# Queries, keys and values as Strassen units of a stage of their own, attention between the gates' products, and down sums that start from nothing

## The chip, the cores and the metric

The kernel runs on one core of a Trainium2 chip. The metric is device time in microseconds, lower is better. Before the change the median of three runs is 2300.4 us (2299.05 to 2302.49).

The engines named in the text: PE multiplies matrices (PEld is its loading of weights), DVE and ACT are the two larger elementwise engines, POOL a smaller one, and SP only issues DMA transfers. Each works through its own instructions in order.

## The reference

One decoder block on 1024 tokens of 1024 features, in fp32:

```python
xn = rmsnorm(x, norm1_g)
qa, ka, va, qr, kr, vr, gr, gate_a, gate_b = [xn @ wl[:, lo:hi] for ...]  # 12 heads of 128 in qa, ka, va
qa, ka = rmsnorm(qa, q_norm_g), rmsnorm(ka, k_norm_g)                      # per head
o_a = mix of three dilated window attentions (4 heads each), weighted by their softmax denominators
o_r = head_groupnorm(retention(qr, kr, vr)) * silu(gr)                     # 4 heads, q and k 256 wide, v 512
y = sigmoid(gate_a) * (o_a @ w_proj_a) + sigmoid(gate_b) * (o_r @ w_proj_b)
x = x + y @ w_out
x = x + square(relu(rmsnorm(x, norm2_g) @ w_up)) @ w_down                  # 4096 wide
```

## The kernel before, in words

**Products.** Each fp32 operand is split in two: h, a copy rounded to a short format (ACT, L319), and l, what is left of it (DVE, L320). A product is then three matmuls, h by h, h by l and l by h (`Pipe.group`, L223). Weights come from DRAM in blocks of 128 x 1024 (`raw`), are split by `Weights.pump`, and keep six pairs of buffers (`wh`, `wl`); a pair is free again when its last product is done (`W.free`).

**Slots.** `Pipe.step` is one slot: the matmuls of one result tile. Small matmuls and transposes that belong to other work are registered with `pipe.at(lag, ...)` and are put between the terms of a later slot ("inserts"). PE's order is the order of the program, written out by hand. The order on the other engines is found by a scheduler when the kernel is built.

**Stages.** (1) Attention: for 12 heads, 8 blocks of 128 tokens each; a step makes q, k and v of one head for one block (8 terms, 24 matmuls of 384 columns), tokens on partitions. q and k are normalised (ACT L651, DVE L332, POOL L333, DVE L655), turned over (two transposes in one insert, L661) and kept in SBUF. Inserts of later slots compute the scores (L585; maximum on DVE L588, exponential on ACT L592), turn them (L598) and multiply them by the values (L605; copied out by ACT, L607). These inserts use the three banks of the PSUM pool `ms`. (2) Gates 0 to 2 as plain products (288 matmuls of 512 columns), beside which DVE makes the sums and differences of x that Strassen's method needs (L715, L718). (3) 21 Strassen units: 5 of gates, 8 of retention's queries and keys, 8 of its swish gates. A unit multiplies in seven products, N1 to N7, of 12 matmuls (`product`); ACT and DVE combine them (L388, L393, L396 on ACT, L398, L403 on DVE), the gates' sigmoid is L690 on ACT, and DVE sums the quarters of the weights (L121). (4) Retention, (5) the projections `w_pa`, `w_pb`, (6) `w_out` with the residual, whose rows are stored to `y_d` in DRAM, (7) the up product and (8) the down product, both by Strassen's method.

**Down sums.** The down product adds its partial products on DVE into eight tiles Y (L1177). Y starts as the residual rows: `load_sums` (L1153) reads them from `y_d`, two tiles while the up product runs and six of 512 KB each at the start of the down product. The finished tiles are stored to `out` by SP in 16 transfers.

Of the kernel before, what the change touches and what calls it, by code (L numbers as in the profile page):

```python
# [17 lines left out]
P = 128  # L18
# [7 lines left out]
RH = 4  # L26
# [11 lines left out]
class Weights:  # L38
# [12 lines left out]
    def __init__(self, nc, rawp, wp, split):  # L51
        self.nc, self.rawp, self.wp, self.split = nc, rawp, wp, split
        self.raw, self.used, self.next = [], set(), 0
        self.src, self.steps = [], []
        self.place, self.more = [], None
# [19 lines left out]
    def add(self, src, buf=None):  # L75
# [17 lines left out]
        self.plain += 1  # L93

# [71 lines left out]
    def load(self):  # L166
# [4 lines left out]
        if any(self.place[m] == b and m not in self.used for m in range(max(0, n - 8), n)):  # L171
            return False
        if b == self.RAW and self.more is None:
            return False
        raw = (self.more if b == self.RAW else self.rawp).tile([P, UW], F, name=f"raw{b}", bufs=1)
# [94 lines left out]
def hybrid_block(ctx: ExitStack, tc: tile.TileContext, a: dict, out: bass.AP):  # L270
# [9 lines left out]
    big = pool(ctx, "big", 4)  # L280
# [14 lines left out]
    v_d = dram.tile([HEADS, S, DH], F, name="v_d")  # L295

    h_d = dram.tile([FF // 512, 2, 4, P, 7, 2, P], F, name="h_d")
    y_d = dram.tile([S, D], F, name="y_d")
# [6 lines left out]
    XS = {(j, i): slot_of(big) for i in range(2) for j in range(2)}  # L305
# [22 lines left out]
    const.tile([P, 224], F, name="rest")  # L328

    def rsqrt(dst, src, scale):  # L330
        w = src.shape[1]
        nc.vector.tensor_scalar(dst, src, scale, EPS, op0=OP.mult, op1=OP.add)  # L332
        nc.gpsimd.tensor_tensor(dst, dst, half[:, :w], op=OP.pow)  # L333
# [7 lines left out]
    for slot, g in heads:  # L341
        for u in range(4):
            W.add(a["w_att"][g * SLOTS + slot, u])
    for d, bufs in enumerate([(0, 1), (2, 4), (3, 5)]):
        for u, b in enumerate(bufs):
            W.add(a["w_gate"][d, u], b)
    NG, NQ = KT - 3, 2 * RH
# [64 lines left out]
    def put_transposed(xn, t, q):  # L412
        pt = tr.tile([P, 4, P], F, name="tr")
        for i in range(4):
            k = 4 * q + i
            nc.tensor.transpose(pt[:, i, :], xn[:, k * P:(k + 1) * P], ident)
        split(*X(slice(4 * q, 4 * q + 4), slice(t * P, (t + 1) * P)), pt)

    def dilated(g, b, src, dst):

        if g == 0:
            return src, dst[:, b * P:(b + 1) * P]
        r = 4 if g == 1 else 8
        src = src.rearrange("p (i r) -> p r i", r=r)
        if g == 1:
            nb, j = divmod(b, 4)
            return src, dst.rearrange("p (r i) -> p r i", r=r)[:, :, nb * P + 32 * j:nb * P + 32 * j + 32]
        return src, dst.rearrange("p (r i) -> p r i", r=r)[:, :, 16 * b:16 * b + 16]

# [61 lines left out]
    attn = ExitStack()  # L491
    p3 = pool(attn, "p3", 2, "right")
    p2 = pool(attn, "p2", 2, "right")
    cpa = pool(attn, "cpa", 1, "right")
    with ExitStack() as ph:
        cp = pool(ph, "cp", 1)
        first = ExitStack()
        px = pool(first, "px", 2)
        cmb = None

        g1 = cp.tile([P, D], F, name="g1")
        gq = cpa.tile([P, HEADS], F, name="gq")
        gk = cpa.tile([P, HEADS], F, name="gk")
        dist = cp.tile([P, 2, 2 * P], F, name="dist")
        row = px.tile([P, D], F, name="xn", bufs=3)
        ones = cp.tile([1, P], F, name="ones")
        xts = {}

        def load_x(t):
            xts[t] = px.tile([P, D], F, name="xt", bufs=3)  # L510
            nc.sync.dma_start(xts[t], a["x"][t * P:(t + 1) * P, :])

        xts[0] = px.tile([P, D], F, name="xt", bufs=3)
        for cs in halves():
# [8 lines left out]
        xn = px.tile([P, D], F, name="xn", bufs=3)  # L523
# [25 lines left out]
        def norm1(t):  # L549
            if t not in xts:  # L550
                load_x(t)
            ss = px.tile([P, 4], F, name="ss")
            xn = px.tile([P, D], F, name="xn", bufs=3)
            nc.scalar.activation(xn, xts[t], AF.Square, accum_out=ss[:, 0:1])
            rsqrt(ss[:, 1:2], ss[:, 0:1], 1.0 / D)
            nc.vector.scalar_tensor_tensor(xn, xts[t], ss[:, 1:2], g1, op0=OP.mult, op1=OP.mult)
            pipe.at(t - 1 - pipe.slot, *[lambda q=q: put_transposed(xn, t, q) for q in range(2)])
# [3 lines left out]
        nc.sync.dma_start(gq, a["q_norm_g"])  # L561
        nc.sync.dma_start(gk, a["k_norm_g"])
        nc.sync.dma_start(dist, a["c_dist"])

        for head, (slot, g) in enumerate(heads):
            h = g * SLOTS + slot
            slope = 2.0 ** (-8.0 * (h + 1) / HEADS)
            us = W.take(4)
            bias = p2.tile([P, 2 * P], F, name="bias")
            qT = p2.tile([P, S], F, name="qT")  # L570
            kT = p2.tile([P, S], F, name="kT")
            V = p2.tile([P, NT, DH], F, name="V")
            Vd = p2.tile([P, NT, DH], F, name="Vd") if g > 0 else V
            acc = p2.tile([P, NT, DH + 2], F, name="acc")

            def attend(g, h, b, bias, qT, kT, V, acc):

                nk = 2 if has_prev(g, b) else 1
                n = nk * P
                k0 = (b + 1 - nk) * P  # L580
                st = {}

                def scores():
                    sp = ms.tile([P, 512], F, name="ms")
                    nc.tensor.matmul(sp[:, :n], qT[:, b * P:(b + 1) * P], kT[:, k0:k0 + n], start=True, stop=True)  # L585
                    s = p3.tile([P, 2 * P], F, name="s")
                    mx = p3.tile([P, 1], F, name="mx")
                    nc.vector.tensor_tensor_reduce(s[:, :n], sp[:, :n], bias[:, 2 * P - n:], op0=OP.add, op1=OP.max,  # L588
                                                   scale=1.0, scalar=-3.0e38, accum_out=mx)
                    nc.vector.tensor_scalar(acc[:, b, DH:DH + 1], mx, -1.0, None, op0=OP.mult)  # L590
                    st["p"] = p3.tile([P, 2 * P], F, name="pr")
                    nc.scalar.activation(st["p"][:, :n], s[:, :n], AF.Exp, bias=acc[:, b, DH:DH + 1],  # L592
                                         accum_out=acc[:, b, DH + 1:DH + 2])

                def turn():
                    tp = ms.tile([P, 512], F, name="ms")
                    for j in range(nk):
                        nc.tensor.transpose(tp[:, j * P:(j + 1) * P], st["p"][:, j * P:(j + 1) * P], ident)  # L598
                    st["t"] = p3.tile([P, 2 * P], F, name="pT")
                    nc.vector.tensor_copy(st["t"][:, :n], tp[:, :n])  # L600

                def values():
# [719 lines left out]
```

## Time and profile before

| | us |
|---|---|
| median of three runs | 2300.4 |
| the profiled execution | 2299.8 |
| its span in the profile | 2297.7 |
| PE busy | 2236.2 |
| DVE busy | 1341.9 |
| ACT busy | 988.0 |
| POOL busy | 103.0 |
| mean granted clock of PE | 0.993 |

In the profile a group of instructions is a line, an engine, an operation and the tiles "out<-in". A wait is written "who <- whom". The attention stage ends near 551 us, the plain gates near 596, the Strassen units near 1000, retention near 1365, the projections near 1596, `w_out` near 1635, the up product near 1985.

### The profile page before, as it was taken

Reading aid. Unit: us, or ns where it says so; the run is one execution under the profiler, and the core shown is the slowest. Engines: PE = TensorE matmul, PEld = TensorE weight load, DVE = VectorE, ACT = ScalarE, POOL = GpSimd, SP = SyncE. Lnnn points to the kernel's source line nnn. Section 1 sums busy time; section 2 is a strip of 40 time slices with the busy share of each in tenths; the row PEclk is TensorE's granted clock in tenths of the full one; section 3 lists DMA queues with packets and bytes.
Section 4 is the critical chain, followed back from the end, with each engine's and each line's share of the span. In section 5 each row is a group of like instructions: output and inputs, shape, how many; then the busy total and the mean of one; then the engine's idle time right before and its main releaser. Section 6 shows DMA issues by size and latency. Waiting matters only on the chain.

```text
span 2297.7 us, 29975 instructions
## 1 busy us (share of the span) xinstructions
PE 2236.2 (97%) x10868; PEld 1915.5 (83%) x10868; DVE 1341.9 (58%) x2588; ACT 988.0 (43%) x2166; POOL 103.0 (4%) x148
## 2 busy tenths in 40 slices
PE   8999999999999999989999999999999999699999
PEld 7999999998888888878888778888787777588887
DVE  6444545455544445548777842453877778777774
ACT  5444435345443333435555533122666667422220
POOL 1111111110000000000000000000000000000000
PEclk9999999999999999999999999999999999899999
DMA  4313132223233333363433484554377789966655
GB/s 146 97 52 114 53 93 93 81 84 101 88 110 110 110 110 110 106 174 111 120 119 101 140 289 152 170 179 142 115 219 230 229 238 277 329 241 261 234 223 201
DMA packets 288805, 353.53 MB, mean 154 GB/s; under 512 B 14609, under 2 KB 215441, under 8 KB 288658
## 3 DMA queue, kind: packets, MB, share of 16 engines
q1 hardware_dynamic: 288658, 351.63, 48.3%
q8 instruction: 85, 1.39, 0.3%
q14 instruction: 62, 0.51, 0.1%
HBM read 229.84 MB, written 121.73 MB: 153 GB/s over the span
## 4 chain that ended last, share of the span: by engine, by line
PE 77%; DVE 8%; DMA 7%; ACT 4%; issue 3%; POOL 0%; SPq 0%; POOLq 0%; ACTq 0%; DVEq 0%
PE mm L223 51%; PE ms L223 20%; DMA raw<-in_w_up 3%; ACT wh L319 2%; DVE wl L320 2%; DMA h_d<-hs 1%; PE ms L605 1%; DVE hs L320 1%; PE ms L585 1%; DVE raw L121 1%; PE tr L661 1%; DVE xl L320 1%; PE ms L598 1%; PE ms L821 1%; DVE u L1120 1%
## 5 line engine op out<-in xcount | busy, mean ns | idle before, releaser
L223 PE MATMUL mm<-wh,xh 128*128 128x384 f32 (+1 forms) x1280 | 503.8, 394 | 0.0
L320 DVE TENSOR_TENSOR wl<-raw,wh 128x1024 fp32r<-128x1024 f32 (+2 forms) x274 | 297.4, 1088 | 298.6 <-ACT wh L319 295.5
L223 PE MATMUL mm<-wh,xl 128*128 128x384 f32 (+1 forms) x1280 | 460.4, 360 | 4.3 <-DVE xl L320 3.2
L223 PE MATMUL mm<-wl,xh 128*128 128x384 f32 (+1 forms) x1280 | 459.2, 359 | 0.0
L319 ACT ACTIVATE wh<-raw 128x1024 fp32r<-128x1024 f32 (+2 forms) x274 | 257.6, 949 | 301.0 <-PE mm L223 77.9
L223 PE MATMUL mm<-xl,wh 128*128 128x512 f32 x848 | 310.0, 390 | 1.7 <-DVE xl L320 1.7
L223 PE MATMUL mm<-xh,wh 128*128 128x512 f32 x848 | 310.5, 391 | 0.0
L223 PE MATMUL mm<-xh,wl 128*128 128x512 f32 x720 | 280.7, 390 | 0.0
L223 PEld LDWEIGHTS mm<-wh,xl 128*128 128x128 f32 x1280 | 241.4, 189 | 27.2 <-DVE xl L320 4.3
L223 PEld LDWEIGHTS mm<-wh,xh 128*128 128x128 f32 x1280 | 242.6, 190 | 21.0 <-ACT ms L1172 0.5
L223 PEld LDWEIGHTS mm<-wl,xh 128*128 128x128 f32 x1280 | 243.4, 190 | 19.1
L223 PE MATMUL ms<-xh,wh 128*128 128x512 f32 x604 | 239.8, 397 | 16.8 <-ACT u L393 13.8
L223 PE MATMUL ms<-xh,wl 128*128 128x512 f32 x604 | 236.0, 391 | 0.0
L223 PE MATMUL ms<-xl,wh 128*128 128x512 f32 x604 | 235.9, 391 | 0.0
L223 PEld LDWEIGHTS mm<-xl,wh 128*128 128x128 f32 x848 | 159.7, 188 | 35.1 <-DVE xl L320 2.1
L223 PEld LDWEIGHTS mm<-xh,wh 128*128 128x128 f32 x848 | 159.7, 188 | 34.0 <-ACT u L396 0.7
L223 PEld LDWEIGHTS mm<-xh,wl 128*128 128x128 f32 x720 | 135.6, 188 | 28.2
L223 PEld LDWEIGHTS ms<-xh,wh 128*128 128x128 f32 x604 | 113.8, 188 | 45.1 <-ACT u L393 18.8
L223 PEld LDWEIGHTS ms<-xh,wl 128*128 128x128 f32 x604 | 113.7, 188 | 24.0
L223 PEld LDWEIGHTS ms<-xl,wh 128*128 128x128 f32 x604 | 113.8, 188 | 22.3
L592 ACT ACTIVATE pr<-s,acc 128x128 f32<-128x128 f32 (+1 forms) x96 | 43.1, 449 | 148.4 <-DVE acc L590 125.5
L1177 DVE TENSOR_TENSOR Y<-Y,ms 128x512 f32<-128x512 f32 x96 | 65.8, 685 | 62.2 <-PE ms L223 62.1
(254 smaller groups left out, 3284.2 us busy)
## 6 DMA issues: line engine op xcount, KB each, us to landing
h_d<-hs SPq DMA_DIRECT2D x112, 512.0 KB, 5.7
xh<-h_d SPq DMA_DIRECT2D x32, 896.0 KB, 5.9
xl<-h_d SPq DMA_DIRECT2D x32, 896.0 KB, 7.2
raw<-in_w_att SPq DMA_DIRECT2D x48, 384.0 KB, 4.0
raw<-in_w_up SPq DMA_DIRECT2D x32, 512.0 KB, 5.1
raw<-in_w_down SPq DMA_DIRECT2D x32, 512.0 KB, 6.0
sg_d<-sg SPq DMA_DIRECT2D x32, 256.0 KB, 2.1
raw<-in_w_rqk_q SPq DMA_DIRECT2D x16, 512.0 KB, 3.7
```

The source lines that it names most:

```text
L121: self.nc.vector.tensor_tensor(x, x, y, op=OP.add)
L223: self.nc.tensor.matmul(ps, x, y, start=start, stop=stop, skip_group_check=not first)
L319: nc.scalar.activation(dst_h, src, AF.Copy)
L320: nc.vector.tensor_tensor(dst_l, src, dst_h.bitcast(F), op=OP.subtract)
L585: nc.tensor.matmul(sp[:, :n], qT[:, b * P:(b + 1) * P], kT[:, k0:k0 + n], start=True, stop=True)
L592: nc.scalar.activation(st["p"][:, :n], s[:, :n], AF.Exp, bias=acc[:, b, DH:DH + 1], accum_out=acc[:, b, DH + 1:DH + 2])
L598: nc.tensor.transpose(tp[:, j * P:(j + 1) * P], st["p"][:, j * P:(j + 1) * P], ident)
L605: nc.tensor.matmul(po[:, :DH], st["t"][:, j * P:(j + 1) * P], V[:, k0 // P + j, :], start=(j == 0), stop=(j == nk - 1))
L661: nc.tensor.transpose(pt[:, j, :], qk[:, j, :], ident)
L821: nc.tensor.matmul(sp[:, :P], kT[:, f], qT[:, f], start=(f == 0), stop=(f == 1))
L1120: nc.vector.tensor_tensor(held[j, x], held[j, x], held[j, y], op=OP.add)
L1177: nc.vector.tensor_tensor(Y[r][:, ns], Y[r][:, ns], ps, op=op)
```

## The change

**A value stage.** The order of the eight token tiles becomes 0, 4, 1, 5, 2, 6, 3, 7. First comes one plain product: the values of the first four heads (8 steps of 24 matmuls of 512 columns). Beside it POOL makes the sums and differences of x, tile by tile (`differences`, 32 operations of 128 x 512), which DVE made in the plain gates. The quarter of x that Strassen's method does not need as an operand (`x01`, 2 MB in its two parts) goes to DRAM and is read back when retention starts.

**A token stage.** The other values and all queries and keys become four Strassen units with tokens on partitions (`add_tokens`, `TOKEN`): 7 products x 4 token tiles x 12 matmuls of 512 columns each. The sums of their weights are made by POOL (32 operations of 128 x 1024), the partial products are combined by ACT and DVE in SBUF, q and k of two heads at a time are normalised (`heads_out`: squares on ACT into PSUM, a reduction on DVE, a power of 128 x 4 and a product of 128 x 512 on POOL), turned over two slots later (`turn_heads`, four transposes in an insert) and written to DRAM (`qk_d`, `v_d`).

**Gates, queries and keys of retention, swish gates** are now all Strassen units, 24 in place of 21. **Attention** runs between their products: block n is begun at slot 4 + 19n/12, with scores, turn and values as inserts at lags 0, 2 and 4. All inserts use the two banks of the pool `tr`. Per pair of blocks SP loads q, k and v and stores the result.

**Down sums.** `y_d` and `load_sums` are gone. `w_out` stores its rows to `out`; of the first chunk, N2, N6, N5 and N4 are copied into Y by ACT; and the finished tiles are added to `out` by 16 DMA transfers that accumulate, issued by POOL.

The core of the diff:

```diff
+    def add_tokens(self, tag, srcs):
...
+            for name, x, need, ends, sums in (
+                    ("N1", "x11", "x11", (), ()), ("N2", "x12", "x12", ("x12",), ()),
+                    ("N6", "x11", "x22", (), (("x22", "x21"), ("x21", "x11"), ("x11", "x22"))),
...
+                            self.nc.gpsimd.tensor_tensor(y, y, z, op=OP.add)
+                        h, l = self.buffer(buf)
+                        self.split(h, l, self.raw[r[x, p]])
...
-    for slot, g in heads:
-        for u in range(4):
-            W.add(a["w_att"][g * SLOTS + slot, u])
...
-    NG, NQ = KT - 3, 2 * RH
+    for u in range(4):
+        W.add(a["w_av"][u])
+    TOKEN = [(("qk", 0), ("v", 1)), (("qk", 1), ("v", 2)), (("qk", 2), ("qk", 3)), (("qk", 4), ("qk", 5))]
...
+    NG, NQ = KT, 2 * RH
...
+        def differences(t):
...
+                nc.gpsimd.tensor_tensor(x[j, i], h.bitcast(F), l.bitcast(F), op=OP.add)
...
+                nc.gpsimd.tensor_tensor(x[v], x[v], x[u], op=op)
+                split(*(y[:, :, cut(t)] for y in operands[name]), x[v])
...
+    def heads_out(u, f, t, c):
...
+        ss = cp.tile([P, 2, 4], F, name="ss")
+        sq = ms.tile([P, 512], F, name="ms")
+        nc.scalar.activation(sq, c, AF.Square)
+        nc.vector.tensor_reduce(ss[:, 0], sq.rearrange("p (a d) -> p a d", a=4), axis=mybir.AxisListType.X, op=OP.add)
+        rsqrt(ss[:, 1], ss[:, 0], 1.0 / DH)
+        c4 = c.rearrange("p (a d) -> p a d", a=4)
+        nc.gpsimd.tensor_tensor(c4, c4, ss[:, 1, :, None].to_broadcast([P, 4, DH]), op=OP.mult)
+        pipe.at(2, lambda: turn_heads(u, f, t, c))
...
+    for u in range(len(TOKEN)):
+        n1, part = {}, {}
+        for name in ("N1", "N2", "N6", "N5", "N3", "N7", "N4"):
+            for t in range(4):
                 pm = mm.tile([P, 512], F, name="mm")
...
+                if name == "N1":
+                    n1[t] = accp.tile([P, 512], F, name="acc")
+                    nc.scalar.activation(n1[t], pm, AF.Copy)
+                elif name == "N2":
+                    c = cp.tile([P, 512], F, name="c")
+                    nc.vector.tensor_tensor(c, pm, n1[t], op=OP.add)
+                    heads_out(u, 0, t, c)
...
+    def attend(n):
...
+        def bank():
+            return tr.tile([P, 4, P], F, name="tr").rearrange("p a b -> p (a b)")
...
+        pipe.at(4, values)
+        pipe.at(2, turn)
+        pipe.at(0, scores)
+
+    def begins(n):
+        return 4 + (n * 19) // 12
...
-        for j, name in strassen_order(NIN):
+        for i, (j, name) in enumerate(strassen_order(NIN)):
+            for fn in at_slot.pop(i, []):
+                fn()
+            mix_next()
             product("in", j, name, unit, operands, lambda: pu, result)
...
+        for i in range(2):
+            nc.sync.dma_start(XS[0, 1][i].bitcast(F), x01_d[i])
...
-                nc.sync.dma_start(y_d[ts, ns], y)
+                nc.sync.dma_start(out[ts, ns], y)
...
-        def load_sums(t, places):
-
-            for r, place in zip((t, t + 4), places):
-                Y[r] = place
-                nc.sync.dma_start(place, y_d[r * P:(r + 1) * P, :])
...
-                nc.vector.tensor_tensor(Y[r][:, ns], Y[r][:, ns], ps, op=op)
+                begun = c > 0 or name in ("N7", "N3")
+                if not begun:
+                    nc.scalar.activation(Y[r][:, ns], ps, AF.Copy, scale=1.0 if op == OP.add else -1.0)
+                else:
+                    nc.vector.tensor_tensor(Y[r][:, ns], Y[r][:, ns], ps, op=op)
                 if last and c == NC - 1:
-                    nc.sync.dma_start(out[r * P:(r + 1) * P, ns], Y[r][:, ns])
+                    nc.gpsimd.dma_start(out[r * P:(r + 1) * P, ns], Y[r][:, ns], accum_op=OP.add)
```

How the instructions move, on two places. First ACT in a Strassen unit of the gates. Before (sg is a gate's sigmoid, wh a split of weights, u and ms are partial products):

```order
L690 ACTIVATE sg<-mm 128x512
L393 ACTIVATE u_6871<-ms 128x512
L396 ACTIVATE u_6886<-mm 128x512
L388 ACTIVATE ms<-mm 128x512
L319 ACTIVATE wh_6919<-raw_6171 128x1024
L690 ACTIVATE sg<-u_6886 128x512
L690 ACTIVATE sg<-u_6871 128x512
L690 ACTIVATE sg<-mm 128x512
L319 ACTIVATE wh_6606<-raw_6774 128x512
L690 ACTIVATE sg<-ms 128x512
```

The same place after (L790 is attention's exponential, L805 the copy of its result out of a bank of `tr`, L719 the sigmoid, L351 a split, L427 and L419 partial products):

```order
L790 ACT_TABLE_LOAD
L790 ACTIVATE s,acc<-s,acc 128x256
L351 ACTIVATE wh_4691<-raw_4374 128x1024
L805 ACTIVATE acc<-tr 128x128
L419 ACTIVATE ms<-mm 128x512
L805 ACTIVATE acc<-tr 128x128
L351 ACTIVATE wh_4806<-raw_4372 128x1024
L719 ACT_TABLE_LOAD
L719 ACTIVATE sg<-u_4743 128x512
L790 ACT_TABLE_LOAD
L790 ACTIVATE s,acc<-s,acc 128x128
```

Exponentials and sigmoids now alternate on ACT, with a load of a function table at each turn; 7 such loads stand in the program before, 85 in the program after. Copies that give banks back stand among them.

Second, the start of the down product, on DVE before (y1b, y1c are places for split weights, L153 sums of weight quarters, hs a stored operand):

```order
L1177 TENSOR_TENSOR Y_15184<-Y_15184,mm 128x512
L320 TENSOR_TENSOR hs<-q_17686,hs 128x512
L1177 TENSOR_TENSOR Y_15185<-Y_15185,ms 128x512
L320 TENSOR_TENSOR y1bl<-raw_17703,y1bh 128x1024
L320 TENSOR_TENSOR y1cl<-raw_17705,y1ch 128x1024
L153 TENSOR_TENSOR raw_17624<-raw_17624,raw_17707 128x1024
L1177 TENSOR_TENSOR Y_17713<-Y_17713,mm 128x512
L153 TENSOR_TENSOR raw_17707<-raw_17707,raw_17705 128x1024
```

and on ACT after (L1276 is the copy into Y, L1269 that of N1 into its bank):

```order
L1276 ACTIVATE Y_14439<-ms 128x512
L1276 ACTIVATE Y_16965<-ms 128x512
L1276 ACTIVATE Y_16966<-mm 128x512
L1269 ACTIVATE ms<-mm 128x512
L1276 ACTIVATE Y_16969<-mm 128x512
L351 ACTIVATE y1bh<-raw_16955 128x1024
L351 ACTIVATE y1ch<-raw_16957 128x1024
L1276 ACTIVATE Y_16966<-ms 128x512
L1276 ACTIVATE Y_16969<-ms 128x512
```

The first sums of a tile have left DVE's queue for ACT's, where two of them stand behind the splits of the same weight blocks.

More of the change, by code (lines that the diff above doesn't have):

```diff
@@ L54, in __init__ @@
         self.src, self.steps = [], []
-        self.place, self.more = [], None
+        self.place, self.more, self.most = [], None, None
         self.last = {}
@@ L1201, in hybrid_block @@
         y1 = pool(sumst, "y1", 1, "right")
[L1203 to L1205 removed]
+        Y.update({r: y1.tile([P, D], F, name=f"Y{r}") for t in (1, 3, 2) for r in (t, t + 4)})
         for x in "abc":
```

470 lines of the change are left out of this document (257 added, 213 removed), and 2 rows, old and new, of the table r.

## The prediction

> **What bounds the kernel now.** First the page's busy times and its clock by slices; then one table by stage (window; length; busy time of PE, its loads, DVE, ACT, POOL; clock; DMA share; GB/s).
>
> ```profile
> PE 2236.2 (97%) x10868; PEld 1915.5 (83%) x10868; DVE 1341.9 (58%) x2588; ACT 988.0 (43%) x2166; POOL 103.0 (4%) x148
> PEclk9999999999999999999999999999999999899999
> ```
>
> ```profile
> 56.00:296.00 240.00, 239.84 (x1492) 234.92 (x1492) 109.90 (x410) 106.58 (x441) 31.02 (x45) 1.00 0.27 79
> 296.00:551.00 255.00, 253.58 (x1538) 243.35 (x1537) 124.20 (x466) 118.16 (x450) 30.64 (x44) 1.00 0.31 91
> 551.00:596.00 45.00, 45.00 (x203) 37.29 (x202) 35.32 (x55) 18.51 (x30) 0.00 (x0) 1.00 0.24 82
> 596.00:1000.00 404.00, 404.00 (x1784) 334.65 (x1783) 186.84 (x231) 152.24 (x214) 0.00 (x0) 1.00 0.36 112
> 1963.00:2013.00 50.00, 30.71 (x119) 23.86 (x117) 34.13 (x42) 17.44 (x24) 0.00 (x0) 0.80 0.99 346
> ```
>
> PE (the matrix engine) works 97% of the span at full granted clock, without a gap in 56 to 296, in 551 to 596 and in 596 to 1000. There, less PE work is time saved and nothing else is. ACT is busy for 152.24 of 404 us (38%) in the Strassen stage, so this stage has room for other work on the small engines. One stretch stands out: 1963 to 2013 has 30.71 us of matmuls in 50 us. The waits of PE (total, times, longest) say why:
>
> ```profile
> PE ms L223 <- DVE Y L1177: 18.2, 2, 15.7
> PE ms L223 <- ACT u L393: 13.8, 10, 3.5
> PE mm L223 <- DVE xl L320: 4.9, 3, 2.1
> ...
> PE ms L585 <- DVE pT L600: 0.9, 2, 0.7
> PE ms L598 <- ACT sg L690: 0.4, 1, 0.4
> PE ms L605 <- ACT sg L690: 0.2, 1, 0.2
> ```
>
> All waits of attention's inserted matmuls (the last three rows) come to 1.5 us in 288 inserts. The one large wait is for the sums Y at the start of the down product: 18.2 us in two waits.
>
> **The change, part by part. 1: the matmuls.** The chain of waits gives the pitch (start, length, what):
>
> ```profile
> 56.56 4.20 PE mm L223 x24
> 60.98 4.18 PE mm L223 x24
> ...
> 190.78 3.13 PE mm L223 x18
> ...
> 317.53 3.13 PE mm L223 x18
> ...
> 596.33 10.88 PE mm L223 x48
> 607.21 2.72 PE ms L223 x12
> ```
>
> 24 matmuls of 384 columns take 4.18 to 4.20 us, 0.1746 each; 48 of 512 take 10.88, 0.2267 each. Removed: 96 steps of 24, 2304 x 0.1746 = 402.2 us. Added: 8 value steps of 24 and 4 units x 7 products x 4 token tiles x 12, together 1536 x 0.2267 = 348.2. Gates 0 to 2 lose 288 matmuls (65.3) and come back as three Strassen units of 84, 252 (57.1). Sum: **-62.2 us**. The inserted transposes and attention matmuls keep their number (q and k go four to an insert, not two): 0, with -4 to +4 for the grouping. The old stage also holds small idle times that go with it: 37.50 - 34.31 = 3.2 us in 18.5 to 56,
>
> ```profile
> 18.50:56.00 37.50, 34.31 (x214) 33.06 (x215) 22.32 (x48) 20.26 (x61) 7.53 (x12) 1.00 0.29 98
> ```
>
> and 255.00 - 253.58 = 1.4 in 296 to 551: **-4.6**. What may come instead is counted below.
>
> **2: the start of the down sums.** The timeline (start, length, engine, line; in brackets the idle time before) around the longest wait:
>
> ```profile
> 1985.22 3.66 SPq L1153 DMA_DIRECT2D Y<-y_d  x6
> 1988.56 1.06 ACT L319 ACTIVATE y1bh<-raw 128x1024 fp32r<-128x1024 f32 x1 [2.26 <-DMA raw<-in_w_down]
> 1989.65 1.23 DVE L320 TENSOR_TENSOR y1bl<-raw,y1bh 128x1024 fp32r<-128x1024 f32 x1 [7.33 <-ACT y1bh L319]
> ...
> 2000.66 0.68 DVE L1177 TENSOR_TENSOR Y<-Y,ms 128x512 f32<-128x512 f32 x1
> ...
> 2001.40 0.80 PE L223 MATMUL ms<-xh 128*128 128x512 f32 x1 [15.72 <-DVE Y L1177]
> ```
>
> Two rows of the DMA issues (number, size, median us to landing) belong to it:
>
> ```profile
> raw<-in_w_down SPq DMA_DIRECT2D x32, 512.0 KB, 6.0
> Y<-y_d SPq DMA_DIRECT2D x8, 512.0 KB, 8.8
> ```
>
> DVE stood for 7.33 us at the split y1bl, which needs a weight block that landed late beside six 512 KB loads of Y; then its other splits and weight sums went first, and only at 2000.66 the addition for which PE had waited 15.72 us. The loads are gone, and 16 of the additions are now ACT copies that need no old Y. Those copies stand on ACT behind the splits y1bh and y1ch (the rows above), which wait for the same weights: so not all of the wait goes. The 50 us stretch holds 119 matmuls, 27 us at the pitch, so 23 us are lost there, the lower clock (0.80) behind the waits among it. If the weights land two to four us sooner and the bank is freed after two ACT splits of 1.06 instead of behind 11 us of DVE work (1989.65 to 2000.66), some 9 of the 23 stay: **-14** (-3 to -20). What is late next there is the transfer of the weights itself.
>
> **3: the small engines in the gates' stage.** A block of attention goes into a stage whose results are sigmoids. The trace shows that alternation once, at the old border (ACT's timeline), and the groups give the other durations:
>
> ```profile
> 547.15 0.18 ACT L592 ACTIVATION_READ_ACCUMULATOR pr<-s,acc 128x1 f32 x1
> 547.35 1.28 ACT L690 ACT_TABLE_LOAD   x1
> 548.64 0.60 ACT L690 ACTIVATE sg<-ms 128x512 f32<-128x512 f32 x1
> ...
> L319 ACT ACTIVATE wh<-raw 128x1024 fp32r<-128x1024 f32 x181 | 189.2, 1056 | 244.5 <-PE mm L223 69.9 <-DMA raw<-in_w_up 55.5 <-DVE raw L121 47.1
> L393 ACT ACTIVATE u<-ms 128x512 f32<-128x512 f32 x37 | 21.9, 591 | 30.7 <-PE ms L223 30.6
> L607 ACT ACTIVATE acc<-ms 128x128 f32<-128x128 f32 x96 | 26.2, 273 | 27.5 <-PE ms L605 26.7
> L592 ACT ACTIVATE pr<-s,acc 128x128 f32<-128x128 f32 (+1 forms) x96 | 43.1, 449 | 148.4 <-DVE acc L590 125.5
> ```
>
> Exp (L592) and Sigmoid (L690) need a table load between them, 1.28 us. Before has 7 loads; the order of the changed kernel has 85, up to 6 to 8 in a unit of gates or of swish gates, hardly any in the query and key units, which have no sigmoid. One such unit: 84 x 0.2267 = 19.0 us of products, and 12/19 of a block in each of its 7 slots, 4.4 blocks. A block's inserts cost PE about 0.87 us: a step of the old stage is (317.53 - 190.78) / 24 = 5.28 us, less 4.19 of products and 0.22 of two transposes (60.98 - 56.56 - 4.20). So a unit lasts 19.0 + 3.8 = 22.8 us. ACT in it: splits 3 x 1.06 + 0.63 = 3.8, copies 3 x 0.59 = 1.8, four sigmoids 2.4, blocks 4.4 x (0.45 + 0.18 + 0.27) = 4.0, six loads 7.7: 19.7 us of 22.8. That is under the bound but no longer idle: 86% against 38%. PE meets ACT in two places. A value insert's bank is freed by an ACT copy, and only two banks ("tr") serve scores, turns, values and the mix; at about 1.9 inserts a slot a bank must be free again 2.7 us after its use. And bank b is freed of N6 by an ACT copy two slots before N7. In ACT's queue an Exp that waits for DVE, or a load and a sigmoid (1.9 us), stands ahead of such copies, and behind a late insert all of PE stands. SP gets 48 x 4 issues here; the store of a pair waits for the last of those ACT copies, and behind it wait weight loads, which land in some 4 us and have a unit's 22.8. Bounds: nothing (the 1.5 us above), or all 78 x 1.28 = 100 us. I take a sixth of that: some 60 late banks at 0.27 us, **+16** (0 to +60), since ACT's sum stays below the unit's time.
>
> **4: the token stage.** Per 2.72 us slot DVE does one to two additions of PSUM (0.685), a reduction and a copy, beside its splits of weights: it fits. New is POOL:
>
> ```profile
> L320 DVE TENSOR_TENSOR wl<-raw,wh 128x1024 fp32r<-128x1024 f32 x181 | 221.1, 1222 | 224.8 <-ACT wh L319 224.3
> L1177 DVE TENSOR_TENSOR Y<-Y,ms 128x512 f32<-128x512 f32 x96 | 65.8, 685 | 62.2 <-PE ms L223 62.1
> L333 POOL TENSOR_TENSOR ssa<-ssa,half 128x2 f32<-128x2 f32 x96 | 66.5, 693 | 427.5 <-DVE ssa L332 410.9 <-DVE w L461 12.2 <-DVE ss L332 4.4
> L332 DVE TENSOR_SCALAR ssa<-ssa 128x2 f32<-128x2 f32 x96 | 16.0, 166 | 38.7 <-ACT junk L651 38.6
> ```
>
> POOL has only powers of two elements in this trace. The nearest rows bound its weight sum of 128x1024: not below DVE's 1.22 us; and, by the ratio of the two engines' smallest operations (0.693 to 0.166, 4.2), not above 5.1. The place that decides is N6, which needs six sums. Their last operand can be loaded once N2 is split, and N2's buffers come free three products (32.6 us) before N6. Two splits and two loads take 12 us, the split after the sums 2.3, four normalisations on POOL between them 8 (a power of 0.7 and a product of 128x512, DVE's 0.685 doubled). At 1.22 us a sum that is 29.6 of 32.6, no wait. At 5.1, with its products as slow, it would be 27 us late, four times. I take 2.0, near the lower row: 34.3, late by 1.7 in each of four units, **+8** (0 to +25).
>
> The Trainium skill, "GPSIMD Engine Reference", section 3.1, has the same operation 1.96 times slower on GpSimd than on DVE, which by DVE's row is an estimate of 2.4 us, 4.1 us late in each unit, and +16 in place of +8; no row of this trace can tell.
>
> **5: the rest.** The value stage starts with 512 KB blocks instead of 384, and waits for the same first tile: **+3** (0 to +8). The token stage's queue must be empty before attention's memory opens, and retention waits behind 2 MB of x: **+3** (0 to +8). At the end 16 accumulating transfers go out on POOL's queue, and read what they add to: **+2** (0 to +6) for the last of them against a plain store of 2.0 us:
>
> ```profile
> out<-Y SPq DMA_DIRECT2D x16, 256.0 KB, 2.0
> ```
>
> **The sum.** Against the profiled execution, 2299.8 us (span 2297.7 and 2.1 around it; the median of three is 2300.4): 2299.8 - 62.2 - 4.6 - 14 + 16 + 8 + 3 + 3 + 2 = **2251.0 us**.
>
> **The rivals.**
> *Nothing new waits.* For it speaks that the old stage put the same 288 inserts between products at 1.5 us of waits. Then 2299.8 - 66.8 - 20 = 2213 to the forecast's lower edge, 2232.
> *ACT becomes the bound.* Its 19.7 us leave 3 a unit. With eight loads (2.6 more) and 3 us of Exp waiting for its maximum in the unit, ACT needs 25.3, 2.5 more than PE; where a late copy also starts the next late bank, double. Over 16 units +40 to +50 in place of +16: 2275 to 2285. Against it: ACT's waits for DVE before Exp were long (148.4 us in 96) only because ACT had nothing else to do.
> *POOL is slow.* At 3.0 us a sum N6 is 7.7 late, 31 in place of 8: 2274; at 5.1 it is 108, 2351.
> *Slower than before: every insert waits for its bank.* In the order of the changed kernel 242 of the 296 inserts come within one slot of the second-last one, whose bank they need. If the engine that empties it is a little late each time, PE pays each time. The other terms leave 2235, so the change loses from 65 / 242 = 0.27 us an insert on; at 0.4 it is 2332. For it: two banks where scores, turns and values had three, and a busier ACT. Against it: two thirds of these banks are emptied by DVE, which was busy for 186.84 of 404 us in 596 to 1000, not by ACT.
> A rule that speaks for this side: ACT's cost of a switch could be longer than the load. In the rows at 547.15 the load starts 0.02 us after the accumulator's read ends, and Sigmoid 0.01 after the load, so a switch costs 1.29; were it twice a load, 2.6, ACT would need 12 + 6 x 2.6 = 27.6 us in a unit with six, 4.8 over, 62 in 13 such units: 2235 + 62 = 2297, about level. The Trainium skill, "ScalarE: Activation LUTs", section "What ACT_TABLE_LOAD costs", has just this: 1283 ns and a drain of 1380 at every switch to another set. The trace agrees with the first figure and shows no drain.
>
> **How the numbers follow.** Forecast, 2232 to 2268: 0.52. Nothing new waits: 0.14. ACT bound, 2268 to 2295: 0.17. POOL slow: 0.06, of which 0.04 below 2295, 0.01 level and 0.01 above. Every insert late: 0.09, of which 0.01 about level. A switch twice as dear: 0.02, level. A measurement of this kernel tells 0.2%, 4.6 us, from no change. Faster: 0.52 + 0.14 + 0.17 + 0.04 = 0.87; same 0.04; slower 0.09. The range goes from 2215 (nearly all hidden) to 2292 (most of the ACT case), and leaves out about 0.03 below and 0.14 above.
>
> **What would show it.** Right: a Strassen stage whose units start 22 to 24 us apart; ACT_TABLE_LOAD some 85 times at 1.28; PE's waits for a bank on ACT's attention copy of 10 to 25 us; token products at 2.72 us with a gap before N6 of some us; the wait for Y at the down start under 9 us, on ACT. Wrong: units of 25 us and more with ACT above 95%; POOL sums over 2.4 us; or PE at a lower granted clock in the new stages, which nothing in this trace lets me expect.

## The result, and the profile after

The changed kernel takes **2317.97 us** (median of 4, 2316.67 to 2321.56) against 2301.0 for the kernel before beside it: ratio 1.0079, 95% interval 1.0064 to 1.0094. It is slower by 0.8%, where 2251 us and faster were forecast. Its profiled span is 2314.9 us, 17.2 more than before.

The page's first rows and PE's clock by slices:

```profile
PE 2212.5 (96%) x10064; PEld 1809.8 (78%) x10064; DVE 1434.6 (62%) x2545; ACT 1087.2 (47%) x1879; POOL 295.8 (13%) x228
PEclk9899998999999999999999999999999999999999
```

PE has 23.7 us less to do (2236.2 before), and POOL 192.8 more (103.0 before). PE's share falls to 96%, and two slices at the start show a lower clock. The table by stage (window; length; busy PE, loads of weights, DVE, ACT, POOL; clock; DMA share; GB/s), cut here at the value stage, the token stage and the gates:

```profile
11.00:84.00 73.00, 60.32 (x249) 45.97 (x248) 47.89 (x50) 31.54 (x55) 50.02 (x38) 0.88 0.41 124
84.00:455.00 371.00, 341.89 (x1524) 278.68 (x1523) 213.73 (x307) 124.05 (x213) 193.76 (x126) 0.94 0.38 112
455.00:1024.00 569.00, 557.25 (x2693) 459.07 (x2692) 327.21 (x834) 357.46 (x642) 5.57 (x4) 0.99 0.50 152
```

The gates' stage is as full as hoped: 557.25 of 569 us. The two new stages are not: 60.32 of 73 and 341.89 of 371, at clocks of 0.88 and 0.94, with POOL at work for two thirds and for half of the time. By the matmuls in them (192 and 1344 at 0.2267) the value stage should last 43.5 us and the token stage 304.7; 16 inserts of four transposes cost 7 us in the one, 48 cost 22.6 (0.47 each, by slots that hold one and no wait) in the other. From the first product of each stage to the first of the next it is 73.4 and 371.5 us. So 23 us are lost in the first, 44 in the second. Retention's first score comes at 1031.9 us; before, it came at 1010.2. That is 21.7 us later in place of the 37 earlier that the forecast's terms give. Behind it the new kernel gains 8.1 between the first turn of the second norm and the last product (698.5 us before, 690.4 after), and loses 4.3 from the last product to the end (4.16 and 8.44).

PE's waits (total, times, longest):

```profile
PE ms L254 <- ACT u L424: 14.0, 10, 3.7
PE tr L642 <- POOL c L675: 9.5, 3, 6.4
PE tr L642 <- POOL acc L675: 8.7, 3, 4.5
PE ms L254 <- ACT xh L351: 8.2, 3, 4.0
PE mm L254 <- DMA xl<-h_d: 6.8, 3, 3.8
PE mm L254 <- ACT acc L694: 6.3, 2, 5.2
...
PE tr L784 <- DMA k<-qk_d: 3.9, 1, 3.9
...
PE tr L784 <- ACT acc L805: 2.7, 3, 1.3
PE tr L796 <- ACT acc L805: 1.9, 2, 1.7
...
PE ms L254 <- ACT Y L1276: 1.0, 1, 1.0
```

The wait for Y is gone (18.2 us before, 1.0 now). New are waits for POOL's product of the normalisation (L675, in two names) and for splits and copies on ACT (L351, L694). They look small beside 67 us; but behind the longer ones PE is slow for some us: matmuls start 0.43 us apart instead of 0.227, as here in the value stage.

```profile
30.70 0.63 PE L254 MATMUL ms<-wh,xh 128*128 128x512 f32 x1 [4.00 <-ACT xh L351]
...
35.18 0.63 PE L254 MATMUL ms<-wl,xh 128*128 128x512 f32 x1
35.61 0.63 PE L254 MATMUL ms<-wh,xl 128*128 128x512 f32 x1
```

The longest is at 100 to 121 us. The timelines of POOL, ACT, DVE and PE there (start, length, engine, line; idle time before in brackets):

```profile
93.84 20.22 POOL L117 TENSOR_TENSOR raw<-raw,raw 128x1024 f32<-128x1024 f32 x7 [7.19 <-DMA raw<-in_w_att_q]
115.31 1.02 POOL L366 TENSOR_TENSOR ss<-ss,half 128x4 f32<-128x4 f32 x1 [1.24 <-DVE ss L365]
116.41 1.04 POOL L675 TENSOR_TENSOR c<-c,ss 128x512 f32<-128x512 f32 x1
117.41 2.38 POOL L117 TENSOR_TENSOR raw<-raw,raw 128x1024 f32<-128x1024 f32 x1
...
111.80 1.06 ACT L351 ACTIVATE wh<-raw 128x1024 fp32r<-128x1024 f32 x1 [4.32 <-POOL raw L117]
...
103.98 2.26 DVE L352 TENSOR_TENSOR wl<-raw,wh 128x1024 fp32r<-128x1024 f32 x1 [3.37 <-ACT wh L351]
106.16 0.68 DVE L697 TENSOR_TENSOR c<-mm,acc 128x512 f32<-128x512 f32 x1
106.77 2.78 DVE L352 TENSOR_TENSOR wl<-raw,wh 128x1024 fp32r<-128x1024 f32 x1
109.47 0.68 DVE L672 TENSOR_REDUCE ss<-ms 128x4 f32<-128x512 f32 x1
112.89 2.27 DVE L352 TENSOR_TENSOR wl<-raw,wh 128x1024 fp32r<-128x1024 f32 x1 [2.74 <-ACT wh L351]
115.07 0.16 DVE L365 TENSOR_SCALAR ss<-ss 128x4 f32<-128x4 f32 x1
...
117.76 2.06 DVE L365 TENSOR_SCALAR ss<-ss 128x4 f32<-128x4 f32 x1
...
106.90 0.80 PE L254 MATMUL mm<-wh,xh 128*128 128x512 f32 x1 [3.81 <-DVE c L697]
117.51 1.12 PE L642 MATMUL tr<-ident,c 128*128 128x128 f32 x4 [6.40 <-POOL c L675]
```

Read it from the end. The transposes at 117.51 waited 6.40 us for POOL's product of 116.41. That product stood in POOL's queue behind seven weight sums, 20.22 us of them. When POOL was free again at 114.06, the power at 115.31 waited 1.24 us more, for DVE's scaling at 115.07 (L365). That scaling stood in DVE's queue behind the split at 112.89, and this one behind ACT's split at 111.80, which had waited 4.32 us for one of POOL's sums. So POOL's queue and DVE's are late together, both by the sums. Beside these sums DVE's split of 128 x 1024, 1.22 us otherwise, takes 2.26 to 2.78, and even a 128 x 4 scaling takes 2.06 (117.76). The reduction at 109.47 reads PSUM (the banks that products land in; the other tiles lie in SBUF), and takes its 0.68 as ever. The addition at 106.16, for which PE waited 3.81 us, came late as well: it stood in DVE's queue behind the split at 103.98, which had waited 3.37 us for ACT's.

POOL's groups (xcount | busy, mean ns | idle before):

```profile
L117 POOL TENSOR_TENSOR raw<-raw,raw 128x1024 f32<-128x1024 f32 x32 | 81.6, 2559 | 68.4 <-DMA raw<-in_w_att_q 54.5 <-DVE ss L365 11.4 <-DVE ss L672 1.7
L366 POOL TENSOR_TENSOR ss<-ss,half 128x4 f32<-128x4 f32 x48 | 60.4, 1258 | 109.9 <-DVE ss L365 106.6 <-PE tr L642 2.6
L675 POOL TENSOR_TENSOR c<-c,ss 128x512 f32<-128x512 f32 x32 | 38.9, 1215 | 2.5
L546 POOL TENSOR_TENSOR x<-x,x 128x512 f32<-128x512 f32 x16 | 26.5, 1658 | 1.1
L543 POOL TENSOR_TENSOR x<-xh,xl 128x512 f32<-128x512 f32 x12 | 16.6, 1395 | 17.0 <-DVE xl L352 17.0
```

### The profile page after: what moved, and what is told of

It is laid out like the page before. It is cut to its first block, busy times and chain, and to the rows that moved or that the text cites. A ratio compares the mean times of both kernels' runs of the same rounds, so it can differ in the third digit from the quotient of the medians.

```text
span 2314.9 us, 28574 instructions
## 1 busy us (share of the span) xinstructions
PE 2212.5 (96%) x10064; PEld 1809.8 (78%) x10064; DVE 1434.6 (62%) x2545; ACT 1087.2 (47%) x1879; POOL 295.8 (13%) x228
## 4 chain that ended last, share of the span: by engine, by line
PE 38%; issue 28%; DVE 1%; DMA 1%; ACT 1%; POOL 1%; SPq 0%; POOLq 0%; DVEq 0%; ACTq 0%
PE mm L254 24%; PE ms L254 10%; PE tr L803 1%; PE tr L784 1%; PE ms L924 1%; PE tr L980 1%; POOL out L1280 1%; DMA pa_d<-s 1%; PE tr L796 0%; DVE xl L352 0%; DMA oraw<-on_d 0%; PE tr L935 0%; ACT xh L351 0%; DMA rkT<-rqk_d 0%; DVE wl L352 0%
## 5 line engine op out<-in xcount | busy, mean ns | idle before, releaser
L352 DVE TENSOR_TENSOR wl<-raw,wh 128x1024 fp32r<-128x1024 f32 (+1 forms) x292 | 341.6, 1171 | 242.7 <-ACT wh L351 234.7
L351 ACT ACTIVATE wh<-raw 128x1024 fp32r<-128x1024 f32 (+1 forms) x292 | 287.1, 986 | 344.8 <-PE mm L254 115.3
L254 PE MATMUL mm<-wh,xh 128*128 128x512 f32 x960 | 392.8, 409 | 13.6 <-ACT acc L694 6.3
L254 PE MATMUL mm<-wh,xl 128*128 128x512 f32 x960 | 380.9, 397 | 3.0 <-DMA xl<-h_d 3.0
L254 PE MATMUL mm<-wl,xh 128*128 128x512 f32 x960 | 380.1, 396 | 0.0
L254 PE MATMUL mm<-xh,wh 128*128 128x512 f32 x896 | 348.1, 412 | 0.0
L254 PEld LDWEIGHTS mm<-wh,xh 128*128 128x128 f32 x960 | 184.0, 192 | 51.1 <-ACT acc L694 7.5
L254 PEld LDWEIGHTS mm<-wh,xl 128*128 128x128 f32 x960 | 184.0, 192 | 44.8 <-DMA xl<-h_d 3.9
L254 PEld LDWEIGHTS mm<-wl,xh 128*128 128x128 f32 x960 | 184.5, 192 | 34.8
L957 POOL TENSOR_TENSOR st<-st,half 128x1 f32<-128x1 f32 x32 | 25.6, 799 | 856.5 <-PE ms L254 579.4
L254 PEld LDWEIGHTS ms<-xl,wh 128*128 128x128 f32 x544 | 103.3, 190 | 17.2
```

The lines of the kernel that those rows point to most:

```text
L254: self.nc.tensor.matmul(ps, x, y, start=start, stop=stop, skip_group_check=not first)
L351: nc.scalar.activation(dst_h, src, AF.Copy)
L352: nc.vector.tensor_tensor(dst_l, src, dst_h.bitcast(F), op=OP.subtract)
L957: nc.gpsimd.tensor_tensor(st[:, 9:10], st[:, 8:9], half[:, 0:1], op=OP.pow)
```

## The experiments

Each run was compared with the kernel before on the same chip; ratios are to that kernel, with their 95% interval. The changed kernel stands at 1.0079. Gains are differences of the medians; by the ratios those against the changed kernel come out 1 to 2 us smaller, as the kernel before took 2301.0 us beside it and 2298.3 to 2298.5 beside the later runs.

**Weight sums on DVE.**

```diff
-                            self.nc.gpsimd.tensor_tensor(y, y, z, op=OP.add)
+                            self.nc.vector.tensor_tensor(y, y, z, op=OP.add)
```

> The 32 weight sums of the token stage (L117, 128x1024) are issued on DVE instead of POOL; nothing else. Theory A (POOL's work sets the token stage: its sums take 2.56 us each, stand ahead of the normalisations in its queue, and stretch DVE's splits): the sums take 1.22 us on DVE, the stalls of the token stage (371.5 us from its first product to its last, against 304.6 of matmuls and some 22 of inserts: 45 us) fall to 15, and the time falls by some 30 us to about 2288. Rival B (the stalls are those of loads and buffers, or DVE is too full to take 39 us more in this stage): the time stays within 8 us of 2318 or rises.

2283.8 us, 0.9937 (0.9920 to 0.9954): 34 us gained, and the losses in the token stage fall from 44 to 9 us. Theory A holds for the sums.

**Differences of x on DVE.**

```diff
-                nc.gpsimd.tensor_tensor(x[j, i], h.bitcast(F), l.bitcast(F), op=OP.add)
+                nc.vector.tensor_tensor(x[j, i], h.bitcast(F), l.bitcast(F), op=OP.add)
...
-                nc.gpsimd.tensor_tensor(x[v], x[v], x[u], op=op)
+                nc.vector.tensor_tensor(x[v], x[v], x[u], op=op)
```

> The 32 sums and differences of x in the value stage (L543, L546, 128x512) are issued on DVE instead of POOL; nothing else. Theory A: they take 0.69 us instead of 1.3 to 1.7, the splits behind them come sooner, DVE's own splits go back from 0.90 to 0.69, and the value stage (73.4 us from its first product, against 43.5 of matmuls and some 7 of inserts) shrinks by 15 to 20 us: about 2300. Rival B (the stage waits for the chain of transposes, splits and differences of a tile whatever engine makes them, and DVE now has 22 us more in it): less than 6 us.

2297.1 us, 0.9995 (0.9984 to 1.0005): 21 us gained, 16.7 of them in the value stage, at the upper end of what A expected.

**Both** edits together.

> Both: weight sums and differences of x on DVE, POOL keeps only the normalisations. Theory A: the two gains add, 45 to 50 us, about 2270, faster than the kernel before. Rival B: no more than the larger of the two alone; if DVE becomes the bound, slower than either.

2267.0 us, 0.9866 (0.9847 to 0.9886). Together they bring 51 us, nearly the sum of the two, and the changed kernel is now 1.3% faster than the kernel before. Retention's first score comes at 980.1 us, 30 earlier than before. Its windows for the same two stages:

```profile
11.00:68.00 57.00, 52.91 (x251) 42.09 (x250) 54.11 (x84) 32.90 (x56) 5.59 (x7) 1.00 0.54 162
68.00:402.00 334.00, 329.00 (x1525) 271.62 (x1524) 227.78 (x338) 122.43 (x211) 113.73 (x92) 0.99 0.42 125
```

52.91 of 57 and 329.00 of 334, at full clock. DVE has more to do in them (54.11 of 57), and the stages are shorter all the same.

**The old down sums** put back (the part of the diff on y_d, load_sums, Y and the stores reversed).

```diff
-                    nc.scalar.activation(Y[r][:, ns], ps, AF.Copy, scale=1.0 if op == OP.add else -1.0)
...
-                    nc.gpsimd.dma_start(out[r * P:(r + 1) * P, ns], Y[r][:, ns], accum_op=OP.add)
+                    nc.sync.dma_start(out[r * P:(r + 1) * P, ns], Y[r][:, ns])
```

> Only the down sums are put back: w_out stores to y_d, Y is loaded from it (eight loads of 512 KB), all additions on DVE, the result stored by SP. From the two traces (retention's last score to the last product is 984.0 us before and 974.5 after; last product to the end 4.1 before and 8.4 after) the new sums are worth 9.5 - 4.3 = 5.2 us: 2323. Theory A (the new sums gain what I forecast, 14 less 2, and something else in the later stages hides half of it): 2330. Rival B (they gain nothing): 2318.

2322.5 us, 1.0102 (1.0087 to 1.0117). That is 4.5 us by the medians and 5.3 by the ratios, close to the 5.2 of the two traces. The intervals just meet, so it is shown that the gain is small, not its last microsecond. The wait for Y is back:

```profile
PE ms L254 <- DVE Y L1281: 19.4, 2, 16.9
```

**One table**: Exp in the place of Sigmoid, for the gates (shown) and the swish gates.

```diff
-        nc.scalar.activation(sg, src, AF.Sigmoid)
+        nc.scalar.activation(sg, src, AF.Exp)
```

> The changed kernel with Exp in the place of every Sigmoid (gates and swish gates; the function is left out, so the output is another one): exponentials and gates then share a table and some 78 table loads, 100 us of ACT, go. Theory A (the gates' stage hides them: PE waits there only 4.6 us for ACT's attention copies): the time falls by 2 to 6 us, 2313. Rival B (ACT's queue sets this stage, as my forecast's +16 and its rival of +45 have it): it falls by 16 or more, 2302 or less.

2305.3 us, 1.0031 (1.0021 to 1.0040): 13 us less, between the two theories. From its first gate product to the end, the gates' stage takes 560.8 us instead of 568.2: the alternation costs 7.4 there, by one trace of each. The other 6 lie behind the gates' stage, in code that the edit does not touch (waits for L424, in the up product, fall from 14.0 to 9.1); why was not found.

**Products of the normalisation on DVE** too, or **on ACT**, on top of both edits:

```diff
-        nc.gpsimd.tensor_tensor(c4, c4, ss[:, 1, :, None].to_broadcast([P, 4, DH]), op=OP.mult)
+        nc.vector.tensor_tensor(c4, c4, ss[:, 1, :, None].to_broadcast([P, 4, DH]), op=OP.mult)
```

> Weight sums, differences of x and the normalisations' products (L675) all on DVE; POOL keeps only the powers. PE still waits 6.4 us for POOL's products in the run with sums and differences on DVE (2267.0). Theory A (POOL's products in its queue are what is left): these waits go, 2261. Rival B (DVE, with 33 us more in the token stage, becomes the one that is late): 2267 or more.

> Weight sums and differences of x on DVE as in e3_both_dve, the normalisations' products on ACT (four of 128x128 for each, scaled by a column) instead of POOL. 192 operations of some 0.36 us, 70 us of ACT in a stage of 320 where ACT is busy for a third. If POOL's product is what transposes wait for: 2261. If ACT's queue then holds the squares and copies back: 2267 or more.

2295.5 us, 0.9987 (0.9974 to 1.0000), and 2294.2, 0.9982 (0.9973 to 0.9991): both give back 27 to 28 us of the gain. PE's waits in the first, and DVE's idle time before its products:

```profile
PE tr L642 <- DVE c L675: 9.7, 10, 1.8
PE tr L642 <- DVE acc L675: 8.1, 5, 4.8
...
L675 DVE TENSOR_TENSOR c<-c,ss 128x512 f32<-128x512 f32 x32 | 22.1, 692 | 30.7 <-POOL ss L366 30.7
```

The times are those of theory B of both, but the trace shows another cause than a DVE or an ACT with too much to do. The product needs POOL's power. On DVE it stands in DVE's queue and waits for that power, 30.7 us before these 32 products and 40.7 us in all (30.7 and 10.0 before the others), and everything behind it on DVE waits with it. In the run on ACT, ACT stands 74.7 us before its products for the same reason, and transposes wait 13.5 us for these and 7.1 for DVE's copies (L655). With the product on POOL, it follows its power there at once (115.31 and 116.41 above). So POOL is the right place for this product as long as the power is made there (means of 1.05 to 1.22 us, two slots ahead), and was the wrong one for the sums. A run with the power off POOL too was not made.

**Idle work on POOL, in the token stage** (on e6_no_pool):

```diff
                         self.split(h, l, self.raw[r[x, p]])
+                        for i in range(4 if self.junk is not None else 0):
+                            cs = slice(256 * i, 256 * i + 256)
+                            self.nc.gpsimd.tensor_tensor(self.junk, h[:, cs].bitcast(F), l[:, cs].bitcast(F), op=OP.add)
```

> The kernel of e6_no_pool and beside it, on POOL, 224 additions of 128x256 in the token stage (four behind each weight split, reading the split weights) whose result nobody reads. Theory A1 (POOL's work costs by itself: a POOL addition and a DVE operation with two SBUF inputs cannot run together): DVE's weight splits of 1.22 us in this stage become 1.6 to 2.0 on average and the time rises by 5 to 20 us over e6_no_pool. Theory A2 (only its place in the chain costed: the sums were slow and others waited for them): the splits stay at 1.22 and the time within 4 us of e6_no_pool.

2362.2 us, 1.0274 (1.0259 to 1.0290): 67 us worse than e6_no_pool, far more than A1 said. But the run does not tell the theories apart. 33 of the 55 splits in the stage lie beside a POOL operation and take 1.43 us on average, the other 22 take 1.22; that is 7 us in all. Most of the loss is another thing, POOL's own queue: the powers stand behind the idle work, DVE's products wait 80.8 us for them instead of 40.7, and PE waits for the products.

```profile
PE tr L648 <- DVE c L681: 43.4, 17, 7.0
L681 DVE TENSOR_TENSOR c<-c,ss 128x512 f32<-128x512 f32 x32 | 25.2, 787 | 69.8 <-POOL ss L370 69.8
```

**Idle work on POOL in the gates' stage** (on e3_both_dve), where next to nothing else is in its queue, behind each split of `add_units`:

```diff
+                for i in range((cols.stop - cols.start) // 200 if self.junk is not None else 0):
+                    cs = slice(200 * i, 200 * i + 200)
+                    self.nc.gpsimd.tensor_tensor(self.junk, h[:, cs].bitcast(F), l[:, cs].bitcast(F), op=OP.add)
```

> e3_both_dve, and on POOL, which is idle in the gates' stage, some 380 additions of 128x200 of split weights (five behind each split of 1024, two behind each of 512) whose result nobody reads, and in whose queue nothing else stands there. Theory A1 (a POOL operation and a DVE operation with two SBUF inputs exclude each other): DVE's splits of 1.22 us and weight sums of 0.69 in this stage come out longer by 0.1 to 0.3 us, exponentials and operands come later, and the time rises by 3 to 20 us. Theory A2 (they do not disturb each other): the same durations as in e3_both_dve to 1% and the same time.

2274.1 us, 0.9889 (0.9874 to 0.9904), 5 to 7 us over e3_both_dve, with intervals that touch; in the traces the stage takes 580.1 us instead of 569.6, and PE waits 19.7 us in it instead of 13.6. POOL's work and DVE's groups of the stage, with it (lines moved by four) and then in e3_both_dve:

```profile
L145 POOL TENSOR_TENSOR rest<-wh,wl 128x200 f32<-128x200 f32 x382 | 266.5, 698 | 275.4 <-DVE wl L356 214.9 <-DVE acc L794 20.8 <-DVE pT L803 6.9
L155 DVE TENSOR_TENSOR raw<-raw,raw 128x512 f32<-128x512 f32 x44 | 40.0, 909 | 0.9
L487 DVE SCALAR_TENSOR_TENSOR oa<-at,w,oa 128x128 f32<-128x128 f32 x48 | 24.0, 523 | 0.7
L803 DVE COPY pT<-tr 128x256 f32<-128x256 f32 x44 | 18.5, 422 | 32.1 <-PE tr L801 32.1
```

```profile
L151 DVE TENSOR_TENSOR raw<-raw,raw 128x512 f32<-128x512 f32 x44 | 30.3, 690 | 0.8
L483 DVE SCALAR_TENSOR_TENSOR oa<-at,w,oa 128x128 f32<-128x128 f32 x48 | 15.6, 349 | 0.7
L798 DVE COPY pT<-tr 128x256 f32<-128x256 f32 x44 | 18.6, 422 | 36.2 <-PE tr L796 36.2
```

Two groups with two inputs in SBUF come out 0.17 to 0.22 us longer on average (0.690 to 0.909, 0.349 to 0.523), the copy out of PSUM not at all (0.422). (The splits, ahead of each piece of POOL work, hardly change, against what A1 expected: 1.224 to 1.248.) Nothing waits for this POOL work. So A1 holds in its main point: POOL's work slows DVE by itself. That PE loses time with it is shown by the stage's length in one trace of each; the times of the whole kernel just fail to tell them apart.

**A version that beats both.** Two Y tiles as before the change, six as in the change:

```diff
-                begun = c > 0 or name in ("N7", "N3")
+                begun = c > 0 or name in ("N7", "N3") or t == 3
...
+                if last and c == NC - 1 and t == 3:
+                    nc.sync.dma_start(out[r * P:(r + 1) * P, ns], Y[r][:, ns])
...
+        for r in (3, 7):
+            nc.sync.dma_start(Y[r], out[r * P:(r + 1) * P, :])
```

> e3_both_dve, and of the eight Y tiles the two that end last (rows 3 and 7) start from the residual as before the change (two loads of 512 KB, additions on DVE) and are stored by SP; the other six keep copies and accumulating transfers. If the 8.4 us from the last product to the end (4.1 before) are the accumulating transfer's, they come back to 4 to 5 and the time falls by 3 to 4 us, to 2263. If they are the price of the last tile itself, nothing changes (2267); if the two loads delay the weights at the down start, it rises to 2270.

2260.2 us, 0.9833 (0.9819 to 0.9846). From the last product to the end it is 4.8 us, 8.0 in e3_both_dve; the spans of the two traces differ by 3.9, the ratios by 7.6 us, of which the tail explains 3.2. The two kinds of transfer stand side by side in this run (number, size, median us to landing):

```profile
out<-Y POOLq DMA_DIRECT2D x12, 256.0 KB, 5.1
out<-Y SPq DMA_DIRECT2D x4, 256.0 KB, 2.1
```

Then attention two slots later, `return 6 + (n * 19) // 12`:

> e9_tail, and attention begins two slots later (slot 6 + 19n/12). PE waits 3.7 to 3.9 us at the first score for keys that have just been written to DRAM; with two slots more (5.4 us) this wait goes: 2 to 4 us faster than e9_tail. If the wait only moves to the next insert: no change.

**2250.8 us, 0.9790 (0.9775 to 0.9805)**, 9 us under e9_tail, where 2 to 4 were expected. The gates' stage takes 560.8 us instead of 566.6: the first wait (3.7 us) and the slow matmuls behind it are gone. The other 3.7 us of the traces lie outside that stage, 2.3 ahead of it and 1.4 behind, where the edit changes no line; they are no gain that this edit is shown to make.

## Why the prediction was wrong

**The matmuls (-62.2): right.** Products keep their pitch: in the new stages, slots without inserts and waits take 2.72 us. With POOL's heavy work moved off, 51 us come back, and retention's first score is 30 us earlier than before, where the forecast's terms give 37: the gain was there. That two more edits then end at the forecast's 2251 is chance, since the forecast had neither of them.

**The token stage (+8): the step that failed.** I took 2.0 us for a weight sum "near the lower row" and counted one late operand a unit. Measured: 2.4 us alone (25 of the 32 take 2.34 to 2.41, the other seven 2.87 to 3.25), 2.56 on average, and 44 us were lost in place of 8. The price alone does not explain it; by my own working 2.56 gives 20 (5.0 us late, four times). Two things were missing. POOL's in-order queue also holds what transposes wait for, behind the sums. (A power of 128 x 4 costs 1.0 to 2.1 us, not 0.7; with its product the pair takes 2.05 at best, as I had priced it, so there the place failed and not the price.) And sums and DVE's operations with two SBUF inputs hold each other up, so that DVE's queue, with the additions that free PSUM banks, is late too. The Trainium skill says so in "SBUF — State Buffer", section "SBUF: two separate sides": the two engines share a pair of ports as an exclusive lock, for DVE operations with two SBUF inputs or in a two-port mode, and the loser waits for the whole instruction. The trace agrees: the scaling at 117.76 ends at 119.82, 0.03 us after the POOL sum that began before it, and in the last idle-work run two-input additions take 0.909 instead of 0.690. (The scaling has one SBUF input; whether it runs in a two-port mode no row shows.) I had left that rule out. The factor of 1.96 to DVE's time (the Trainium skill, "GPSIMD Engine Reference", section 3.1) agrees as well: 2.40 / 1.22 = 1.97. Two of my three signs of being wrong were there, sums over 2.4 us and a lower clock in the new stages (0.88 and 0.94). I wrote that nothing let me expect the second, though 0.80 behind the long wait for Y stood in my own table.

**The value stage (+3): failed in the same way.** My term had larger blocks in it and a first tile. The 32 operations on POOL that the change puts there had no price at all; they take 1.3 to 1.7 us each, and ACT's splits wait for them:

```profile
L351 ACT ACTIVATE xh<-x 128x512 fp32r<-128x512 f32 x36 | 22.6, 631 | 37.8 <-POOL x L546 26.4 <-DVE x L1131 4.6 <-DVE x L1135 4.2
```

23 us were lost, and 16.7 came back with these operations on DVE.

**The gates' stage (+16): the size about right, partly by luck.** PE's waits between 455 and 1024 are 11.7 us in all, 4.6 of them for the attention copy on ACT, for which I had 10 to 25; 3.9 are for keys from DRAM, which no term had. Units come 23.6 us apart on average, as forecast. Table loads number 85 (82 in these rows), and what idle time stands before them is almost all a wait for DVE's maximum before Exp:

```profile
L790 ACT ACT_TABLE_LOAD x40 | 51.3, 1283 | 13.5 <-DVE acc L789 11.5 <-issue 1.4
L719 ACT ACT_TABLE_LOAD x23 | 29.5, 1283 | 1.5 <-DMA sg_d<-sg 1.1
L843 ACT ACT_TABLE_LOAD x19 | 24.4, 1283 | 1.4 <-DMA sr_d<-sg 1.1
```

100 us of loads on ACT cost PE 7.4. The drain of 1380 ns that the Trainium skill ("ScalarE: Activation LUTs", "What ACT_TABLE_LOAD costs") adds to a switch is not there: 1.5 us of idle time before 23 loads. The rivals fall: ACT is no bound (357.46 of 569 us, 63%), and the bank of an insert is late for 4.9 us in 288 attention inserts, 0.02 each, not 0.27.

**The down sums (-14 and +2): mechanism right, sizes off.** In the traces they are worth 8.1 - 4.3. The wait for Y went, but 14 us of the stretch's losses stay (I said 9): the same 280 matmuls, 63.5 us at the pitch, took 87.1 us before and 77.6 after. PE now waits for operands that the up product has just stored, 7.8 us in four waits, and not for weights. The longest is:

```profile
2032.69 0.79 PE L254 MATMUL mm<-y1ah,xl 128*128 128x512 f32 x1 [3.79 <-DMA xl<-h_d]
```

The loads of `xl` just ahead of it stand on SP behind four issues of weight blocks (2019.72 to 2025.15), so the weights may still have a part in it; no run shows how large. By these traces the terms that were too good, 36 us in the token stage, 20 in the value stage and 8 in the down sums, make up 64 of the 67 us between forecast and measurement.

**The rival "POOL is slow"** named the place and had 0.06. It was the case; its own prices (31 us at 3.0 a sum) were too low for the same reason, and it left the value stage out.

## What to carry to other kernels

Work moved to a slow engine that is "idle" has three prices: its own duration, everything behind it in that engine's queue, and what it does to DVE's operations on SBUF tiles meanwhile. Price each operation that a change puts on POOL, in every stage, and ask what stands behind it before asking whether the engine has time. Heavy two-input sums of SBUF tiles beside a busy DVE are dearer on POOL than on that same busy DVE; a product with two slots of slack is well placed there, next to the power that it needs. A short step that stays on a slow engine makes whoever reads it stand still, and on an in-order engine all that follows.

## What was not expected of the hardware

A DVE scaling of 128 x 4, 0.16 us, takes up to 2.25 us beside a POOL sum: that an operation is short does not protect it. Of the DVE operations beside POOL's work in the rows above, only those that read PSUM keep their time. Transfers that accumulate into DRAM from POOL's queue end 3 to 5 us later than SP's plain stores at the end of the kernel (7.6 to 9.4 us from the last product in the nine runs that have them there, 4.2 to 4.8 in the four with plain stores); whether the accumulation or POOL's queue is to blame, no run separates. Not settled: how the token stage's 44 us divide between POOL's queue and the blocking of DVE, and why the run without sigmoids gains 6 us behind the gates. The order on ACT, DVE and POOL is found anew by the scheduler for each run, so each experiment also carries what that changed.
